# Another order of the Strassen products and down tiles, and the band sums behind two down tiles, in a two-layer hybrid trunk

## The chip, the cores and the metric

The kernel runs as one program on one core of a Trainium2 chip. The metric is the device time of one execution in microseconds (us), as the median of several. One execution is also recorded by the profiler; all rows below come from that one.

## What is computed

640 tokens (128 context, 512 latent) of width 1024 go through two layers. Each layer is a mixing part and a dense feed-forward part (FFN), each between two RMS norms with scale, shift and gate from a conditioning vector. Layer 0 mixes by attention and a state space scan, layer 1 by a pooling mixer. What matters here is the FFN, the pooling mixer, and the gate rows:

```python
def modulation(cvec, w_mod, b_mod):
    m = jnp.expand_dims(jax.nn.silu(cvec) @ w_mod + b_mod, -2)
    return split_last(m, (D_MODEL,) * 6)

def swiglu(h, w_gate, w_up, w_down):
    return (jax.nn.silu(h @ w_gate) * (h @ w_up)) @ w_down

# pool_mixer: mean over a window of 2, 4, 8 or 16 tokens, less the token,
# then one 256x256 product for each quarter of the width
    xp = xp + g_p * rmsnorm(mix_p, norm_post_mix[l])
    fp = swiglu(modulate(xp, norm_pre_ffn[l], shf_p, scf_p), ffn_w_gate[l], ffn_w_up[l], ffn_w_down[l])
    xp = xp + gf_p * rmsnorm(fp, norm_post_ffn[l])
```

The FFN is 1024 to 2816 and back. All is float32 in and out.

## The kernel before

Float32 products are made of three matmuls: each operand is split into a high part (tiles named `h..`, or `ah`, `a1h`, by a ScalarE copy, L89 and L588) and a low part (`l..`, `al`, `a1l`, a subtraction, L90 and L589), and high by high, high by low and low by high are summed in PSUM. `net.split` (L86) does it for weights: ScalarE the high part, VectorE (or the engine handed over) the low part. `net.raw` (L71) takes a buffer of a ring of four, named "raw", and loads 128x1024 of a weight into it over the SyncE queue.

`_ffn` (L517) works on 22 tiles of the hidden width, in 11 pairs of a gate and an up matrix. The first pair is "plain": eight products (L97 to L99) whose weights are split up front, low parts on GpSimd, with the last tiles of the work before (`tails`) put between. The other 20 matrices (L514) use a scheme of seven products with half-size operands, p1 to p7, each of 12 matmuls with 320 columns. Products 1, 6, 7 and 4 add up in one PSUM tile A, products 5 and 3 in a tile B; between the steps of A, ScalarE copies what is there (L548 after p1, L558 after p6, L566 after p7), so p6 has to wait for L548, p7 for L558 and p4 for L566. While one matrix is multiplied, the next is prepared: `load` (SyncE), `adds` (four sums on GpSimd, L484 to L487, of two raw tiles into `q` and `t4`), and the splits `a`, `b`, `c`, `d`. Between products stand five calls `d()`: each multiplies one tile of 128 tokens of the pair before with half of its down weights (six matmuls with 512 columns; L97 to L99, added up on VectorE at L611), and lets the background generators go on by a step (`net.bg`). `out_split` (L588, L589) splits the finished hidden tile, on ScalarE and GpSimd.

The background work, `mod_gate_mac`, makes gate rows that are wanted later: for each half it takes four units of 512 KB of `w_mod` through the ring and multiplies and adds them on VectorE (L273, four instructions a unit; "MAC" below). The first FFN has four such halves, the second two.

After the first FFN's loop, `finish0` runs: the last two pairs' down products (`tail`, 48 matmuls for a pair of 128-token tiles, 24 for one), post-norm (`finish_tile`), next pre-norm into `hn`, and the pooling mixer: `pool_in(tt)` multiplies `hn` by a band matrix on TensorE (L1348), `mix(tt)` by the pool weights (L1650) and makes the next pre-norm, whose transposes (L331) lie in `trs`. `_band_shift` (L1363 reduction on VectorE, L1365 a tiny matmul, L1368 eight scalings) makes the shift for `pool_in` out of the band, which is loaded over the ScalarE queue when `finish0` starts.

The code hands instructions to a tile framework that orders those of each engine by its own planning; the order in the code is where it starts from. Every engine runs its own queue; the queue of SyncE carries the weight loads.

Of the kernel before, what the change touches and what calls it, by code (L numbers as in the profile page):

```python
# [9 lines left out]
F32 = mybir.dt.float32  # L10
# [7 lines left out]
P = 128  # L18
# [27 lines left out]
class Net:  # L46
# [211 lines left out]
    def mod_gate_mac(self, dst, l, j, half, gain):  # L258
        nc = self.nc
# [5 lines left out]
        nc.scalar.dma_start(gb, self.t[gain][l, c0 : c0 + 512].partition_broadcast(P))  # L265
        acc = self.mrp.tile([P, 2, 512], F32, tag="macc", name=self.name("macc"), bufs=1)
        for u in range(4):
            x = self.raw(self.t["w_mod"][l, 2 * j + half, u])
            yield
            for k2 in range(2):  # L270
                kc = 2 * u + k2
                for v in range(2):
                    nc.vector.scalar_tensor_tensor(  # L273
                        acc[:, v], x[:, k2 * 512 : k2 * 512 + 512], self.silc[:, kc, v : v + 1],
                        acc[:, v] if kc else bb, op0=ALU.mult, op1=ALU.add,
                    )
                if k2 == 0:
                    yield
        for v in range(2):
            h = self.mrp.tile([P, 512], F32R, tag="modh", name=self.name("modh"), bufs=1)  # L280
            lo = self.mrp.tile([P, 512], F32R, tag="modl", name=self.name("modl"), bufs=1)
# [187 lines left out]
class Matrix:  # L469
# [28 lines left out]
    def d(self, eng=None):  # L498
        self.wd = self.net.split(self.fr, "d", self.t4, eng)
# [17 lines left out]
def _ffn(net, l, A, fr, sp, tails, switch, finish):  # L517
    nc, t = net.nc, net.t
# [73 lines left out]
    def down_load(q, dh):  # L592
        return net.raw(t["w_down"][l, q, dh])
# [19 lines left out]
    g0, u0 = mats(0)  # L613
    g0.load()
    u0.load()
    w0 = {}
    for f in range(2):
        for m, tags in ((g0, "ab"), (u0, "cw")):
            w0[m, f] = net.split(fr, tags[f], (m.ra, m.rb)[f], nc.gpsimd)
    s0 = sp.tile([P, 2, TOK], F32, tag="sg", name=net.name("sg"))  # L620

    def plain(m, f, half):
        out = net.pt([P, HB])
        wh, wl = (x.rearrange("p (k n) -> p k n", k=KC) for x in w0[m, f])
        net.mm3(out, [(wh[:, k], wl[:, k], bh, bl) for k, (bh, bl) in enumerate(A.plain(half))])
        d = s0[:, f, half * HB : half * HB + HB]
        if m is g0:
            nc.scalar.activation(d, out, AF.Silu)
        else:
            nc.vector.tensor_tensor(d, d, out, ALU.mult)  # L630

    plain(g0, 0, 0)
    tails.pop(0)()
    plain(u0, 0, 0)
    tails.pop(0)()
    plain(g0, 1, 0)
    plain(u0, 1, 0)
    plain(g0, 0, 1)
    A.pair(0, 64)
# [23 lines left out]
    for n, m in enumerate(seq, 2):  # L663
        p, up = divmod(n, 2)
        w = Work(m, wg if up else None)
# [8 lines left out]
        def d():  # L674
            if fill:
                down_add(fill.pop(0), up, [(prev, wdn)], p == 1)
            net.bg()
# [4 lines left out]
        w.p2()  # L682
        if final and up:
            last[1, 0] = net.split(fr, "a", down_load(NPAIR - 1, 0), None)
        w.p6()
        d()
        w.p5()
        if nx:
            nx.a()
        w.p7()  # L690
        if nx:
            nx.adds()
# [2 lines left out]
            nx.c()  # L695
        if final and up:
            last[0, 1] = net.split(fr, "c", down_load(NPAIR - 2, 1), None)
        w.p4()
        if up:
            at = [out_split(wg, 0)]  # L700
# [4 lines left out]
        if nx:  # L705
            nx.b()
            nx.d()
        d()
        d()
        if up:  # L710
            if final:
                last[1, 1] = net.split(fr, "b", down_load(NPAIR - 1, 1), None)
# [662 lines left out]
def trunk(ctx: ExitStack, tc: tile.TileContext, t: dict, o: dict):  # L1375
    net = Net(ctx, tc, t, o)
    nc = tc.nc
# [14 lines left out]
    with pool("x0", "right", 2) as xp:  # L1392
# [4 lines left out]
        for tt in range(NT):  # L1397
            x = xp.tile([P, D], F32, tag="x", name=net.name("x"), bufs=NT)
            net.in_dma(tt, x)
            xts.append(x)  # L1400
        a, _ = net.mod_ab_of(0, None, sc, PV_PREMIX)
# [109 lines left out]
    with pool("xg", "right") as xg, pool("wo", "left") as wo:  # L1511
# [31 lines left out]
        for tt in range(NT):  # L1543
# [6 lines left out]
            x = xq.pop(0)  # L1550
# [72 lines left out]
    def finish0(tail, right):  # L1623
# [7 lines left out]
        nc.scalar.dma_start(band, t["band"])  # L1631
        us = pool_weights()
        a = net.mod_ab_of(1, m1[0], m1[1], PV_PREMIX)[0]
        ab = a, _band_shift(net, band, m1[0])
        abf = net.mod_ab_of(1, m1[3], m1[4], PV_PREFFN)
        pfs, trs = {}, []

        def pool_in(tt):
            pfs[tt] = _pool_tile(net, pp, band, hn, tt, ab)

        def mix(tt):
# [21 lines left out]
        def rest():  # L1663
            pool_in(3)
            mix(2)
            trs.pop(0)()
            pool_in(4)
            mix(3)
            trs.pop(0)()
            mix(4)  # L1670
            trs.pop(0)()
            return trs

        return rest
# [122 lines left out]
```

## Time and profile before

| | |
|---|---|
| median of 3 runs | 1468.32 us (1464.43 to 1470.96) |
| the profiled execution | 1471.61 us |
| its span in the trace | 1469.7 us |
| TensorE (PE) busy | 1382.8 us, 94% of the span, 7914 matmuls |
| VectorE (DVE) busy | 1008.8 us, 69% |
| ScalarE (ACT) busy | 642.0 us, 44% |
| GpSimd (POOL) busy | 449.2 us, 31% |
| mean granted clock of TensorE | 0.965 of full |

TensorE is busy nearly all the time, so the rest of the span, some 87 us, is what waits on it add up to, and a granted clock below 1 is time that its matmuls take longer. Of the two levels 0.5 is 1.2 GHz and 1.0 is 2.4 GHz. A figure between them for a stretch is a mean. Brackets at the end of a timeline row give the idle time of that engine just before the instruction and what released it.

### The profile page before, as it was taken

What the parts mean: (1) busy time and instruction counts of PE and PEld (TensorE: products, weight loads), DVE (VectorE), ACT (ScalarE), POOL (GpSimd) and SP (SyncE); (2) the same over time, 40 slices, a digit from 0 to 9 for tenths busy, and PEclk for the clock granted to TensorE, in tenths of its full rate; (3) what the DMA queues carried; (4) which work ended last, traced back from release to release, by engine and by line L of the source; (5) the groups of instructions that cost most, each with busy time, mean ns of one, the idle gap of its engine ahead of it and who ended that gap; (6) DMA issues with size and microseconds to landing.
All of it is one profiled execution on the core that took longest, in us unless ns stands there. A gap on an engine that the chain in (4) does not pass through costs nothing.

```text
span 1469.7 us, 20410 instructions
## 1 busy us (share of the span) xinstructions
PE 1382.8 (94%) x7914; PEld 1181.7 (80%) x7914; DVE 1008.8 (69%) x1460; ACT 642.0 (44%) x1138; POOL 449.2 (31%) x357
## 2 busy tenths in 40 slices
PE   5999999999998989899999998697999999999998
PEld 2888765667567978798899998597998899999996
DVE  3755547777747886887876666476878766666657
ACT  3545634744325544333333434256553333433443
POOL 0000133354300544335253333022442433333320
PEclk9999999999999999999999999787999999999999
DMA  9433435600063242333232224321242332222213
GB/s 366 134 129 126 139 136 188 201 29 1 29 215 115 94 142 81 115 122 115 94 129 87 87 86 144 130 86 43 66 134 91 113 115 86 87 87 79 79 58 143
DMA packets 50276, 165.45 MB, mean 113 GB/s; under 512 B 5938, under 2 KB 9522, under 8 KB 50052
## 3 DMA queue, kind: packets, MB, share of 16 engines
q1 hardware_dynamic: 43344, 153.96, 31.1%
q10 hardware_dynamic: 6836, 10.19, 2.1%
q8 instruction: 62, 1.02, 0.3%
q14 instruction: 34, 0.28, 0.1%
HBM read 155.57 MB, written 8.56 MB: 112 GB/s over the span
## 4 chain that ended last, share of the span: by engine, by line
PE 45%; DVE 10%; issue 4%; POOL 4%; DMA 3%; ACT 2%; POOLq 0%; DVEq 0%; ACTq 0%; SPq 0%
PE ps L514 25%; PE ps L99 6%; PE ps L97 6%; PE ps L98 6%; DVE macc L273 3%; PE ps L1348 2%; POOL al L589 1%; PE ps L1650 1%; DVE a2l L421 1%; DMA raw<-in_w_mod 1%; DMA band<-in_band 1%; DVE y L611 1%; DVE la L90 1%; POOL q L484 1%; POOL q L485 1%
## 5 line engine op out<-in xcount | busy, mean ns | idle before, releaser
L484 POOL TENSOR_TENSOR q<-raw,raw 128x512 f32<-128x512 f32 x40 | 57.8, 1444 | 389.1 <-DVE lc L90 207.5
L99 PE MATMUL ps<-hw,al 128*128 128x512 f32 x380 | 151.8, 399 | 4.1 <-POOL al L589 4.0
L611 DVE TENSOR_TENSOR y<-y,ps 128x512 f32<-128x512 f32 x180 | 120.8, 681 | 50.3 <-PE ps L99 49.6
L97 PE MATMUL ps<-hw,ah 128*128 128x512 f32 x380 | 152.3, 401 | 0.0
L98 PE MATMUL ps<-lw,ah 128*128 128x512 f32 x380 | 152.1, 400 | 0.1
L514 PE MATMUL ps<-a2h,hc 128*128 128x320 f32 x320 | 101.2, 316 | 11.0 <-ACT sg L548 11.0
L589 POOL TENSOR_TENSOR al<-sg,ah 128x640 fp32r<-128x640 f32 x42 | 75.7, 1806 | 94.9 <-ACT ah L588 94.9
L514 PE MATMUL ps<-a2h,lc 128*128 128x320 f32 x320 | 101.1, 316 | 0.0
L514 PE MATMUL ps<-a2l,hc 128*128 128x320 f32 x320 | 100.9, 315 | 0.0
L514 PE MATMUL ps<-a2h,hb 128*128 128x320 f32 x320 | 99.0, 309 | 0.0
L514 PE MATMUL ps<-a1h,ha 128*128 128x320 f32 x320 | 98.9, 309 | 0.0
L514 PE MATMUL ps<-a1h,la 128*128 128x320 f32 x320 | 98.8, 309 | 0.0
L514 PE MATMUL ps<-a1l,ha 128*128 128x320 f32 x320 | 98.8, 309 | 0.0
L514 PE MATMUL ps<-a2l,hb 128*128 128x320 f32 x320 | 98.8, 309 | 0.0
L514 PE MATMUL ps<-a2h,lb 128*128 128x320 f32 x320 | 98.8, 309 | 0.0
L90 DVE TENSOR_TENSOR lc<-q,hc 128x1024 fp32r<-128x1024 f32 x40 | 51.2, 1279 | 60.7 <-ACT hc L89 60.7
L99 PEld LDWEIGHTS ps<-hw,al 128*128 128x128 f32 x380 | 72.4, 190 | 23.4 <-POOL al L589 6.1
L89 ACT ACTIVATE hc<-q 128x1024 fp32r<-128x1024 f32 x40 | 42.4, 1059 | 96.2 <-PE ps L514 79.2
L98 PEld LDWEIGHTS ps<-lw,ah 128*128 128x128 f32 x380 | 72.6, 191 | 10.8 <-DVE lw L90 0.5
L97 PEld LDWEIGHTS ps<-hw,ah 128*128 128x128 f32 x380 | 72.7, 191 | 10.2
L273 DVE SCALAR_TENSOR_TENSOR macc<-raw,silc,macc 128x512 f32<-128x512 f32 x84 | 74.4, 923 | 5.6 <-DMA raw<-in_w_mod 5.6
L89 ACT ACTIVATE hb<-raw 128x1024 fp32r<-128x1024 f32 x44 | 46.6, 1060 | 66.4 <-issue 33.4
(449 smaller groups left out, 4010.3 us busy)
## 6 DMA issues: line engine op xcount, KB each, us to landing
raw<-in_w_mod SPq DMA_DIRECT2D x80, 512.0 KB, 3.8
raw<-in_w_gate SPq DMA_DIRECT2D x44, 512.0 KB, 3.6
raw<-in_w_up SPq DMA_DIRECT2D x44, 512.0 KB, 3.7
raw<-in_w_down SPq DMA_DIRECT2D x44, 512.0 KB, 4.3
mraw<-in_w_mod SPq DMA_DIRECT2D x16, 512.0 KB, 10.2
xs<-xd SPq DMA_DIRECT2D x10, 512.0 KB, 8.3
x<-in_x_sample SPq DMA_DIRECT2D x8, 512.0 KB, 7.5
raw<-in_w_xbc SPq DMA_DIRECT2D x8, 512.0 KB
```

Of the source, the lines that this page charges most:

```text
L89: self.nc.scalar.activation(h, x, AF.Copy)
L90: (eng or self.nc.vector).tensor_tensor(l, x, h.bitcast(F32), ALU.subtract)
L97: mm(out, ah, bh, start=first and i == 0, stop=False)
L98: mm(out, ah, bl, start=False, stop=False)
L99: mm(out, al, bh, start=False, stop=last and i == n - 1)
L273: nc.vector.scalar_tensor_tensor(acc[:, v], x[:, k2 * 512 : k2 * 512 + 512], self.silc[:, kc, v : v + 1], acc[:, v] if kc else bb, op0=ALU ...
L421: eng.tensor_tensor(l, x, h.bitcast(F32), ALU.subtract)
L484: g.tensor_tensor(self.q[:, lo], self.rb[:, lo], self.ra[:, lo], ALU.subtract)
L514: mm(out, x[:, k], z[:, k], start=first and n == 0, stop=n == len(terms) - 1, skip_group_check=True)
L589: (eng or nc.gpsimd).tensor_tensor(al, g.s[:, f], ah.bitcast(F32), ALU.subtract)
L611: nc.vector.tensor_tensor(yd, yd, out, ALU.add)
L1348: nc.tensor.matmul(o, x, m, start=i == 0, stop=i == len(mats) - 1, skip_group_check=True)
```

## The change

Five edits. The seven products and five down tiles stand in another order: before p1 p2 p6 d p5 p7 d p4 d p3 d d, now p1 p2 p5 p6 d d p7 d p4 d p3 d (the splits of the next matrix keep their places among them, but for `a`, `b` and `d`). The gate rows' units have a buffer of their own, one (`mraw`), and give control back once before their first MAC more and once more behind the last. The first pair's four splits are made one by one, ahead of the product that needs them, with low parts on VectorE. `_band_shift` is called by the first `pool_in`, after the tails of two tiles. In `rest`, the third set of transposes stands ahead of `mix(4)`.

```diff
--- before.py
+++ after.py
@@ -265,7 +265,9 @@
         nc.scalar.dma_start(gb, self.t[gain][l, c0 : c0 + 512].partition_broadcast(P))
         acc = self.mrp.tile([P, 2, 512], F32, tag="macc", name=self.name("macc"), bufs=1)
         for u in range(4):
-            x = self.raw(self.t["w_mod"][l, 2 * j + half, u])
+            x = self.mrp.tile([P, 1024], F32, tag="mraw", name=self.name("mraw"), bufs=1)
+            nc.sync.dma_start(x, self.t["w_mod"][l, 2 * j + half, u])
+            yield
             yield
             for k2 in range(2):
                 kc = 2 * u + k2
@@ -274,8 +276,7 @@
                         acc[:, v], x[:, k2 * 512 : k2 * 512 + 512], self.silc[:, kc, v : v + 1],
                         acc[:, v] if kc else bb, op0=ALU.mult, op1=ALU.add,
                     )
-                if k2 == 0:
-                    yield
+                yield
         for v in range(2):
             h = self.mrp.tile([P, 512], F32R, tag="modh", name=self.name("modh"), bufs=1)
             lo = self.mrp.tile([P, 512], F32R, tag="modl", name=self.name("modl"), bufs=1)
@@ -614,9 +615,10 @@
     g0.load()
     u0.load()
     w0 = {}
-    for f in range(2):
-        for m, tags in ((g0, "ab"), (u0, "cw")):
-            w0[m, f] = net.split(fr, tags[f], (m.ra, m.rb)[f], nc.gpsimd)
+
+    def first(m, f, tag):
+        w0[m, f] = net.split(fr, tag, (m.ra, m.rb)[f])
+
     s0 = sp.tile([P, 2, TOK], F32, tag="sg", name=net.name("sg"))
 
     def plain(m, f, half):
@@ -629,11 +631,15 @@
         else:
             nc.vector.tensor_tensor(d, d, out, ALU.mult)
 
+    first(g0, 0, "a")
     plain(g0, 0, 0)
+    first(u0, 0, "c")
     tails.pop(0)()
     plain(u0, 0, 0)
+    first(g0, 1, "b")
     tails.pop(0)()
     plain(g0, 1, 0)
+    first(u0, 1, "w")
     plain(u0, 1, 0)
     plain(g0, 0, 1)
     A.pair(0, 64)
@@ -682,11 +688,12 @@
         w.p2()
         if final and up:
             last[1, 0] = net.split(fr, "a", down_load(NPAIR - 1, 0), None)
+        w.p5()
         w.p6()
-        d()
-        w.p5()
         if nx:
             nx.a()
+        d()
+        d()
         w.p7()
         if nx:
             nx.adds()
@@ -695,6 +702,7 @@
             nx.c()
         if final and up:
             last[0, 1] = net.split(fr, "c", down_load(NPAIR - 2, 1), None)
+        d()
         w.p4()
         if up:
             at = [out_split(wg, 0)]
@@ -705,8 +713,6 @@
         if nx:
             nx.b()
             nx.d()
-        d()
-        d()
         if up:
             if final:
                 last[1, 1] = net.split(fr, "b", down_load(NPAIR - 1, 1), None)
@@ -1631,11 +1637,13 @@
         nc.scalar.dma_start(band, t["band"])
         us = pool_weights()
         a = net.mod_ab_of(1, m1[0], m1[1], PV_PREMIX)[0]
-        ab = a, _band_shift(net, band, m1[0])
+        ab = [a]
         abf = net.mod_ab_of(1, m1[3], m1[4], PV_PREFFN)
         pfs, trs = {}, []
 
         def pool_in(tt):
+            if len(ab) == 1:
+                ab.append(_band_shift(net, band, m1[0]))
             pfs[tt] = _pool_tile(net, pp, band, hn, tt, ab)
 
         def mix(tt):
@@ -1667,8 +1675,8 @@
             pool_in(4)
             mix(3)
             trs.pop(0)()
+            trs.pop(0)()
             mix(4)
-            trs.pop(0)()
             return trs
 
         return rest
```

In the changed kernel the line numbers move by 1 to 8 (L548 becomes L549, L588 becomes L589, L273 becomes L275, L1363 becomes L1369).

ScalarE, at the border between two pairs of the first FFN: `ah` are the high parts of the pair that is done, L548 the copy of A after p1 of the next matrix. Before:

```order
L588 ACTIVATE ah_5890<-sg_5583 128x640
L290 DMA gd<-macc_5383 1x512
L89 ACTIVATE hb_5925<-raw_5772 128x1024
L265 DMA gb_5942<-in_npost_mix 128x512
L588 ACTIVATE ah_5921<-sg_5583 128x640
L89 ACTIVATE hw_5961<-raw_5959 128x1024
L548 ACTIVATE sg_5965<-ps_5970 128x320
L264 DMA bb_6474<-in_b_mod 1x512
```

Now:

```order
L89 ACTIVATE hd_5915<-t_1086_5839 128x512
L589 ACTIVATE ah_5879<-sg_5556 128x640
L89 ACTIVATE hw_5921<-raw_5919 128x1024
L89 ACTIVATE hb_5911<-raw_5743 128x1024
L549 ACTIVATE sg_5925<-ps_5930 128x320
L589 ACTIVATE ah_5907<-sg_5556 128x640
L89 ACTIVATE ha_5985<-raw_5926 128x1024
```

The copy after p1 (now L549) has moved ahead of the second `ah`, and the down weights' `hw` ahead of `hb`.

VectorE, at the end of the first FFN: the low parts of the last pair, then the additions of the tails (`y<-y,ps`), the band's reduction, and `hn` of tile 0. Before:

```order
L90 TENSOR_TENSOR lb_8370<-raw_8367,hb_8369 128x1024
L589 TENSOR_TENSOR al_8364<-sg_8121,ah_8363 128x640
L1363 TENSOR_REDUCE rs_8423<-band 128x4
L1368 TENSOR_SCALAR mv_8427<-mv_1567,ps_8425 128x2 x8
L611 TENSOR_TENSOR y<-y,ps_8437 128x512
L350 TENSOR_TENSOR junk_8451<-y,G_8379 128x512
L352 TENSOR_SCALAR ss_1494_8452<-ss_1494_8452 128x1
```

Now, from the third addition of the tails on:

```order
L351 TENSOR_TENSOR junk_8488<-y,G_8379 128x512
L353 TENSOR_SCALAR ss_1491_8439<-ss_1491_8439 128x1
L612 TENSOR_TENSOR y<-y,ps_8494 128x512
L351 TENSOR_TENSOR junk_8488<-y,G_8379 128x512
L1369 TENSOR_REDUCE rs_8524<-band 128x4
L105 RECIPROCAL r_8462<-sd_8461 128x1
L1374 TENSOR_SCALAR mv_8528<-mv_1567,ps_8526 128x2
L365 SCALAR_TENSOR_TENSOR xs_8385<-junk_8438,r_8462,xs_8385 128x512 x2
L353 TENSOR_SCALAR ss_1502_8489<-ss_1502_8489 128x1
L1374 TENSOR_SCALAR mv_8528<-mv_1567,ps_8526 128x2 x7
L105 RECIPROCAL r_8470<-sd_8469 128x1
L316 TENSOR_SCALAR hn<-xs_8385,r_8470 128x1024
```

The reduction moved from ahead of the first addition to behind the fourth, and stays ahead of `hn`.

VectorE, in the first gate matrix of the first FFN: MACs of the second and third unit (`raw_4958` and `raw_5002` before, `mraw_4974` and `mraw_5128` now). Before:

```order
L273 SCALAR_TENSOR_TENSOR macc_4881<-raw_4958,silc,macc_4881 128x512 x4
L90 TENSOR_TENSOR lc_4932<-q_4915,hc_4931 128x1024
L273 SCALAR_TENSOR_TENSOR macc_4881<-raw_5002,silc,macc_4881 128x512
L567 TENSOR_TENSOR sg_4821<-sg_4821,ps_4884 128x320
L273 SCALAR_TENSOR_TENSOR macc_4881<-raw_5002,silc,macc_4881 128x512 x3
L90 TENSOR_TENSOR ld_4979<-t_943_4916,hd_4978 128x512
```

Now:

```order
L90 TENSOR_TENSOR la_4882<-raw_4822,ha_4881 128x1024
L90 TENSOR_TENSOR lc_4940<-q_4923,hc_4939 128x1024
L275 SCALAR_TENSOR_TENSOR macc_4898<-mraw_4974,silc,macc_4898 128x512 x4
L568 TENSOR_TENSOR sg_4821<-sg_4821,ps_4855 128x320
L275 SCALAR_TENSOR_TENSOR macc_4898<-mraw_5128,silc,macc_4898 128x512 x3
L90 TENSOR_TENSOR ld_4995<-t_944_4924,hd_4994 128x512
```

Between the last MAC of one unit and the first of the next stood a split (`lc`); now a short addition stands there.

## Rows read from the trace of the kernel before

**Rows 1.** Stages: us; busy PE, PEld, DVE, ACT, POOL; clock, DMA share, GB/s.

```profile
560.00:754.00 194.00, 182.43 (x1034) 166.51 (x1033) 156.64 (x191) 70.21 (x101) 80.43 (x48) 0.97 0.34 110
754.00:908.00 154.00, 154.00 (x928) 144.32 (x927) 97.19 (x116) 61.41 (x87) 51.53 (x38) 1.00 0.31 99
1040.00:1150.00 110.00, 105.22 (x622) 97.41 (x620) 90.61 (x101) 49.68 (x72) 47.37 (x29) 0.98 0.35 114
```

**Rows 2.** Waits of PE, whole span: waiting, releaser, total us, times, longest.

```profile
PE ps L1365 <- DVE rs L1363: 14.4, 1, 14.4
PE ps L514 <- ACT sg L548: 11.0, 4, 4.9
PE ps L97 <- DVE a1h L431: 7.6, 1, 7.6
...
PE ps L97 <- ACT ha L89: 3.6, 1, 3.6
```

**Rows 3.** Waits of PE, 545 to 760 us (first FFN, MAC stretch).

```profile
PE ps L514 <- ACT sg L566: 4.1, 2, 3.1
PE ps L514 <- ACT sg L548: 4.0, 2, 2.1
PE ps L99 <- POOL al L589: 3.3, 3, 1.5
```

**Rows 4.** Timeline, ACT, 598 to 617 us: start, length, operation [idle, releaser].

```profile
601.62 0.74 ACT L588 ACTIVATE ah<-sg 128x640 fp32r<-128x640 f32 x1 [3.74 <-DVE sg L579]
...
603.21 0.42 ACT L548 ACTIVATE sg<-ps 128x320 f32<-128x320 f32 x1
```

**Rows 5.** Timeline, DVE, 582 to 610 us.

```profile
600.77 0.81 DVE L579 TENSOR_TENSOR sg<-sg,sg 128x640 f32<-128x640 f32 x1
```

**Rows 6.** Timeline, POOL, 560 to 705 us.

```profile
581.77 1.29 POOL L484 TENSOR_TENSOR q<-raw,raw 128x512 f32<-128x512 f32 x1 [16.90 <-DMA raw<-in_w_gate]
```

**Rows 7.** Page, part 5: busy us, mean ns, idle before with its releaser.

```profile
L589 POOL TENSOR_TENSOR al<-sg,ah 128x640 fp32r<-128x640 f32 x42 | 75.7, 1806 | 94.9 <-ACT ah L588 94.9
...
L90 DVE TENSOR_TENSOR lc<-q,hc 128x1024 fp32r<-128x1024 f32 x40 | 51.2, 1279 | 60.7 <-ACT hc L89 60.7
```

**Rows 8.** Table by stage, the 10 us around one wait of the MAC stretch.

```profile
610.00:620.00 10.00, 6.87 (x30) 5.74 (x29) 8.18 (x10) 2.96 (x5) 2.88 (x2) 0.83 0.35 109
```

**Rows 9.** Page, part 6: DMA issues, count, KB each, us to landing.

```profile
raw<-in_w_mod SPq DMA_DIRECT2D x80, 512.0 KB, 3.8
```

**Rows 10.** Waits of PE, 1040 to 1400 us (second FFN).

```profile
PE ps L514 <- ACT sg L548: 2.1, 1, 2.1
PE ps L514 <- ACT sg L566: 2.0, 2, 1.6
```

**Rows 11.** Timeline, PE, between the two FFNs.

```profile
928.24 0.59 PE L1365 MATMUL ps<-rs,cm 128*128 128x4 f32 x2 [14.45 <-DVE rs L1363]
...
945.63 1.60 PE L1348 MATMUL ps<-band,hn 128*128 128x128 f32 x12 [3.11 <-DVE hn L315]
```

**Rows 12.** Timeline, DVE, 912 to 948 us.

```profile
917.76 0.81 DVE L589 TENSOR_TENSOR al<-sg,ah 128x640 fp32r<-128x640 f32 x1
927.50 0.69 DVE L1363 TENSOR_REDUCE rs<-band 128x4 f32<-128x512 f32 x1 [8.93 <-DMA band<-in_band]
...
942.56 0.69 DVE L611 TENSOR_TENSOR y<-y,ps 128x512 f32<-128x512 f32 x1
```

**Rows 13.** Timeline, POOL, 960 to 1024 us.

```profile
970.95 2.81 POOL L90 TENSOR_TENSOR la<-raw,ha 128x1024 fp32r<-128x1024 f32 x1
```

**Rows 14.** Table by stage, between the two FFNs.

```profile
914.00:928.00 14.00, 0.00 (x0) 0.00 (x0) 5.04 (x5) 1.47 (x2) 2.76 (x2) 0.60 0.96 355
...
946.00:978.00 32.00, 32.00 (x181) 27.88 (x180) 26.30 (x47) 19.66 (x48) 9.45 (x4) 1.00 0.16 52
```

**Rows 15.** Timeline, ACT, 510 to 522 us.

```profile
518.20 0.74 ACT L588 ACTIVATE ah<-sg 128x640 fp32r<-128x640 f32 x1 [2.67 <-DVE sg L630]
```

**Rows 16.** Timeline, PE, 1000 to 1022 us.

```profile
1007.68 1.89 PE L1650 MATMUL ps<-q,pf 128*128 128x256 f32 x8
```

## The prediction

> **What bounds the kernel now.** I read the waits of TensorE first, then a table by stage, then the queues of the engines that TensorE waits for. The table [rows 1] shows two kinds of stretch inside the same loop over matrices. Between 754 and 908 us TensorE is busy for all of 154.00 us at full clock (1.00); between 560 and 754 us, the same loop with background multiply-accumulates (MACs, L273) on VectorE beside it, it is busy for 182.43 of 194.00 us at 0.97, and VectorE works 156.64 us there. So the loop has nothing to give where VectorE is light, and the time to be had lies in its waits. These are few [rows 2]: 14.4 us once for the band sums, 11.0 us in four waits for the copy L548 (the longest 4.9), 7.6 us once for the first operand of layer 1's FFN, 3.6 us for the first weight of layer 0's. In the first MAC stretch they are 4.1, 4.0 and 3.3 us [rows 3], 11.4 in all.
>
> How such a wait arises: ScalarE stood 3.74 us for the low-priority `ah` of the pair just ended, and the copy that TensorE wanted (L548, after p1) came behind it, at 603.21 us [rows 4]. `ah` waited for VectorE's L579 at 600.77 us [rows 5], late behind MACs. Upstream of it, GpSimd's sums for the next matrix once stood 16.90 us for a weight load [rows 6]: the MAC loads share four buffers with the weights.
>
> **The change, part by part.** The sum is made against the profiled execution (1471.61 us), which lies 3.3 us above the median, so 3.3 comes off at the end.
>
> *Order of products, first FFN.* TensorE does the same matmuls, so nothing is added; what moves is who is late. In the new ScalarE order the copy after p1 stands ahead of the second `ah`, so p6 no longer hangs on L579, and p5 runs before p6 too: the 4.0 us [rows 3] should go. For L566, 4.1 us, the new order puts two down tiles instead of one between the copy and p4 (six more matmuls, under 1.7 us by the 13.7 us of 48 tail matmuls below), and the weights' buffers are freer; I take half, 2.0. For `al` I take nothing: counted from the end of p3, the first down tile that reads it used to follow two old down tiles and three products and now follows four products, so it comes rather earlier, while a low part takes 1.81 us on GpSimd [rows 7]. Each wait also leaves a restart: a window of 10 us with one shows a granted clock of 0.83 instead of 1.00 [rows 8], so 3.4 us at half rate, which costs 1.7; three windows of this stretch show it, 5.1 in all, of which I take 3.0 with the waits. Sum 9; bounds 2 (the L548 waits are half filled by what is late next, `al`) and 16.5 (11.4 and 5.1).
>
> *Modulation rows in their own buffer, more background steps.* This adds and removes no MAC; per half 22 steps instead of 14 spread 16 MACs. It frees the ring of four for weights, which is what [rows 6] waits for. But one buffer serves all units, so a unit's load starts only after the last MAC of the unit before it. A load takes 3.8 us to land [rows 9]. The VectorE rows of the first gate matrix show four MACs of one unit and three of the next with one short addition between: there VectorE will stand for about 3.8 us, once in each FFN. VectorE is 81% busy in such a stretch [rows 1], so most of it is slack; in other places splits and additions stand between. The SyncE queue also holds weight loads behind a waiting MAC load; the weights are wanted a matrix later, so I cost it at nothing; if that cover is gone, GpSimd's sums are late next, then `hc`, then p5.
>
> *Second FFN's MAC stretch.* Its waits are 2.1 and 2.0 us [rows 10], half as many MACs, VectorE 90.61 of 110 us [rows 1]. By the same shares: 2.1 and 0.9 of restart, 3. Bounds 0 and 6.
>
> *Band sums behind two down tiles.* Now TensorE's queue has the little matmul L1365 ahead of the tails; it waits for the band's load, and TensorE stands 14.45 us, to 928.24 [rows 11]. The reduction itself starts when the band has landed, 927.50 [rows 12]. In the new order the tails need only the last low part, which ended at 917.76 + 0.81 = 918.6 [rows 12]. Before, 48 tail matmuls took from 928.8 to the last addition at 942.56 [rows 12], 13.7 us with their half-rate start; nine of them now run ahead of the end of p3, so 39 are left: 11.1 us, last addition at about 929.7. VectorE's new order puts the reduction and the eight scalings behind that addition and ahead of `hn` of tile 0, so after it come its product (0.7), the reduction (0.69), matmul, update of x, square and `hn`: about 6.5 us against 3.1 before (945.63 less 942.56 [rows 11, 12]). pool_in(0) starts at 936.2 rather than 945.6: 9.4 less. The nine early matmuls push the end of p3 by 1.6 (2.1 less 0.5 into a wait), and the new 6.5 us of idle time before pool_in(0) brings one more restart, 1.7. I take 6. Bounds: 2 (the restart lasts over pool_in(0) and its neighbours) and 11 (`hn` not held up by the reduction). Its cover for the load of the band: the tails; without them the old 14.45 is back.
>
> That `hn` waits its turn is why 6.5 and not 3.1 is counted. VectorE stood 8.93 us at the reduction [rows 12] and ran nothing behind it; but nothing behind it was ready then, so the row alone doesn't decide. The Trainium skill, Perfetto Trace Analysis, section Tensor Engine Instruction, says that ScalarE, VectorE and GpSimd start their instructions strictly in order. By that rule the band brings 6; without it 6 + 3.4, about 9.
>
> *First splits one by one, on VectorE.* Low parts go from GpSimd (2.81 us each beside VectorE [rows 13]) to VectorE (1.28 [rows 7]). In the second FFN's start TensorE is busy throughout that stretch (946 to 978 us, 32.00 of 32.00 [rows 14]), so nothing. At the first FFN's start TensorE waited 3.6 [rows 2] for `ha`, which I leave; the 4.9 for L548 came from an `ah` at 518.20 [rows 15] ahead of it. It goes, but `al` of that same tensor is wanted by the first down tile about 2.5 us later. I take 3; bounds 0 and 5.
>
> *Transposes ahead of mix(4).* TensorE's wait of 7.6 [rows 2] comes because the last transposes stood behind mix(4), whose first eight matmuls take 1.89 [rows 16], all sixteen about 3.6. Moved, mix(4) fills 3.6 of the wait and the operand comes 3.6 sooner; but its ScalarE and VectorE work then meets the first plain products. I take 2: bounds 7.6 (all of it) and -4 (mix(4) at half rate and its work in the operand's way).
>
> Sum 9 + 3 + 6 + 3 + 2 = 23: 1448.6 in the terms of the profiled run, **1445** on the median. Its own range: 1437 to 1453.
>
> **Rivals.** (a) *Waits move instead of going*: VectorE has no less to do, and the next late row (`al`, L566) takes over. Then the loops bring 3 together, the band 5, the starts 0: 1463.6, 1460 on the median. For it: 156.64 of 194 us. Against: the stall followed above came from the order of ScalarE's queue. (b) *All MAC waits and restarts go*, as in the quiet stretch: 16.5 + 6 + 6 + 3 + 2 = 33.5: 1435. For it: a ring free of MAC loads; against: MACs are still bunched. (c) *`hn` overtakes the reduction*: 3.4 more, 1442; against it the VectorE order. (d) *Slower by the clock*: pool_in(0) now starts after idle time; if the clock then stays at half over the 32.00 us of work that had 1.00 [rows 14], 32 us come back: 1480.6 less 3.3, 1477. It decides from 23 us at half. Against: before, it was full in that stretch although TensorE had done nothing from 914 to 928 us [rows 14]. (e) *Slower by the single buffer*: if all 24 units cost VectorE 3.8 us, the first stretch's 16 take 61 of its 37 free us and the second's 8 take 30 of its 19; 35 us fall on TensorE, the loops' 12 don't come, 11 remain: 1495.6, 1492 on the median; it decides from 2.8 us for each unit. Against: in most places two or more splits stand between units. (f) *Nothing moves*: 1468.
>
> **Numbers.** Forecast 0.45, (a) 0.22, (b) 0.13, (c) 0.05, (d) 0.06, (e) 0.05, (f) 0.04. About 0.5%, 7.3 us, is what a measurement of this kernel can tell from no change: faster means below 1461. Forecast, (b), (c) and most of (a) lie there, 0.80; the rest of (a) and (f) 0.12; (d), (e) 0.08. The range goes from 1431, under (b), to 1462, over (a).
>
> **What would show it.** Right: no wait of TensorE on the band reduction; its tails start some 5 us after p3; a wait of 5 to 7 us for `hn`; no p6 wait on `ah`; MAC stretches near 1.00. Wrong: MACs with idle time released by the modulation load, weight loads late behind them, half clock past 936 us, or a 7 us wait still at the second FFN's start.

## The result, and the profile after

The changed kernel takes 1448.39 us (median of 4 runs, 1447.63 to 1449.88), beside 1469.64 us of the kernel before (4 runs): a ratio of 0.9862, 95% interval 0.9834 to 0.9890. The profiled execution took 1448.13 us, 23.5 less than the profiled one before. The forecast was 1445, with a range of 1431 to 1462. So the total came out close, but the parts that made it did not: that is what this section and the runs below show.

TensorE's busy time fell from 1382.8 to 1370.3 us with the same 7914 matmuls, at a mean granted clock of 0.978 instead of 0.965. So of the 23.4 us by which the span shrank, 12.5 are busy time that shrank, and 10.9 are waits that went.

Waits of TensorE in the changed kernel, whole span (waiting, releaser, total us, times, longest), to be laid beside [rows 2]:

```profile
PE ps L515 <- ACT sg L549: 12.2, 5, 6.4
...
PE ps L332 <- DVE y L316: 4.3, 2, 2.7
PE ps L1354 <- DVE hn L316: 4.3, 1, 4.3
PE ps L97 <- DVE a1h L432: 4.1, 1, 4.1
PE ps L97 <- ACT ha L89: 3.6, 1, 3.6
PE ps L99 <- POOL al L590: 3.3, 4, 0.9
PE ps L1371 <- DVE rs L1369: 3.2, 1, 3.2
```

The wait for the band sums is down from 14.4 to 3.2 us, and 4.3 for `hn` have come; the wait for the second FFN's operand went from 7.6 to 4.1, with 4.3 for `y` (the transposes) new beside it. The wait of p6 for the copy after p1, which was to go, has grown from 11.0 to 12.2.

Where the 23.5 us came from is read at landmarks that both programs have: the start of p1 of the first and of the 19th matrix in each FFN's loop, and the start of the first pool tile (945.63 and 917.69 us). Times are differences of start times in the two timelines.

| stretch | before, us | after, us | change | forecast |
|---|---|---|---|---|
| start to first matrix of the first FFN's loop | 510.7 | 506.3 | -4.4 | -3 |
| first FFN's loop, 18 matrices | 377.3 | 365.0 | -12.3 | -9 |
| 19th matrix to the first pool tile | 57.6 | 46.4 | -11.2 | -6 |
| first pool tile to the second FFN's loop | 107.1 | 104.8 | -2.3 | -2 |
| second FFN's loop, 18 matrices | 356.5 | 362.2 | +5.7 | -3 |
| the rest, to the end of the execution | 62.4 | 63.4 | +1.0 | 0 |

Stages after (us; busy PE, PEld, DVE, ACT, POOL; clock, DMA share, GB/s), to be read beside [rows 1]: the MAC stretch of the first FFN, the quiet one behind it, and the first matrices of the second FFN.

```profile
555.00:750.00 195.00, 192.14 (x1125) 176.58 (x1124) 147.91 (x182) 72.08 (x106) 71.54 (x51) 1.00 0.33 106
750.00:890.00 140.00, 139.74 (x837) 130.38 (x836) 101.34 (x127) 57.56 (x83) 48.61 (x33) 1.00 0.33 107
1030.00:1130.00 100.00, 95.25 (x537) 87.42 (x538) 70.45 (x83) 43.32 (x65) 38.03 (x28) 0.97 0.31 101
```

The MAC stretch is nearly quiet now: 192.14 of 195.00 us busy at clock 1.00, where it was 182.43 of 194.00 at 0.97. Its waits, of which three groups of [rows 3] had added up to 11.4 us, are these (two more are of 0.6 and 0.3):

```profile
PE ps L99 <- POOL al L590: 0.9, 1, 0.9
PE ps L515 <- DVE sg L568: 0.6, 1, 0.6
...
PE ps L515 <- ACT sg L549: 0.4, 1, 0.4
```

The second FFN's loop is the loss. Its first two matrices took 26.9 and 22.0 us, where they had taken 20.3 and 20.0, 8.6 more; the other 16 took 2.9 less. The first FFN's first matrix shows the same thing, 28.3 us, where it had taken 27.1. ScalarE there:

```profile
509.73 1.05 ACT L89 ACTIVATE hw<-raw 128x1024 fp32r<-128x1024 f32 x1
517.36 0.23 ACTq L264 DMA_DIRECT2D bb<-in_b_mod  x1
517.64 0.44 ACT L549 ACTIVATE sg<-ps 128x320 f32<-128x320 f32 x1 [6.86 <-POOL bb L263]
```

ScalarE's queue came to a load of 2 KB of bias (L264, for the second half of the gate rows), and stood 6.86 us; the copy after p1 (L549), which p6 of TensorE waited for, was the next behind it. The load waited for a memset on GpSimd:

```profile
508.77 2.29 POOL L485 TENSOR_TENSOR q<-raw,raw 128x512 f32<-128x512 f32 x1
...
514.36 2.51 POOL L488 TENSOR_TENSOR t<-raw,q 128x512 f32<-128x512 f32 x1
516.81 0.52 POOL L263 MEMSET bb<- 128x512 f32 x1
```

The memset itself takes 0.52 us; it stood behind four sums for the next matrix. The prediction had weighed what the copy would no longer stand behind, and not what else had moved in front of it. In the second FFN the same chain costs 4.6 us where before there was no such wait. GpSimd and ScalarE of the changed kernel:

```profile
1029.64 0.52 POOL L263 MEMSET bb<- 128x512 f32 x1
1030.55 1.06 ACT L89 ACTIVATE hw<-raw 128x1024 fp32r<-128x1024 f32 x1 [6.56 <-POOL bb L263]
```

and GpSimd of the kernel before:

```profile
1044.88 0.53 POOL L263 MEMSET bb<- 128x512 f32 x1 [3.75 <-DVE a2l L421]
```

Before, the memset stood ahead of the four sums, the first of which started at 1049.86; now it stands behind them (1021.04 to 1029.69).

### The profile page after: what moved, and what is told of

Read it like the earlier page. It is cut to its first block, busy times and chain, and to the rows that moved or that the text cites. A ratio compares the mean times of both kernels' runs of the same rounds, so it can differ in the third digit from the quotient of the medians.

```text
span 1446.3 us, 20387 instructions
## 1 busy us (share of the span) xinstructions
PE 1370.3 (95%) x7914; PEld 1172.8 (81%) x7914; DVE 984.5 (68%) x1468; ACT 639.0 (44%) x1140; POOL 415.9 (29%) x349
## 4 chain that ended last, share of the span: by engine, by line
PE 74%; DVE 10%; DMA 6%; issue 4%; ACT 3%; POOL 2%; POOLq 0%; ACTq 0%; DVEq 0%; SPq 0%
PE ps L515 26%; PE ps L97 11%; PE ps L99 11%; PE ps L98 11%; DMA mraw<-in_w_mod 3%; PE ps L179 3%; DVE macc L275 3%; PE ps L1354 2%; PE ps L1255 1%; PE ps L1658 1%; PE ps L1237 1%; DMA band<-in_band 1%; PE ps L1217 1%; PE ps L1238 1%; PE ps L1239 1%
## 5 line engine op out<-in xcount | busy, mean ns | idle before, releaser
L485 POOL TENSOR_TENSOR q<-raw,raw 128x512 f32<-128x512 f32 x40 | 54.9, 1372 | 362.7 <-DMA raw<-in_w_up 117.2
L99 PE MATMUL ps<-hw,al 128*128 128x512 f32 x380 | 151.2, 398 | 1.8 <-POOL al L590 1.8
L612 DVE TENSOR_TENSOR y<-y,ps 128x512 f32<-128x512 f32 x180 | 121.1, 683 | 39.1 <-PE ps L99 36.5
L515 PE MATMUL ps<-a2h,hc 128*128 128x320 f32 x320 | 100.8, 315 | 12.2 <-ACT sg L549 12.2
L275 DVE SCALAR_TENSOR_TENSOR macc<-mraw,silc,macc 128x512 f32<-128x512 f32 x84 | 79.3, 972 | 28.0 <-DMA mraw<-in_w_mod 28.0
L488 POOL TENSOR_TENSOR t<-raw,q 128x512 f32<-128x512 f32 x40 | 58.5, 1464 | 100.0 <-DVE ld L90 65.8
L98 PEld LDWEIGHTS ps<-lw,ah 128*128 128x128 f32 x380 | 72.2, 190 | 12.2
L89 ACT ACTIVATE hd<-t 128x512 fp32r<-128x512 f32 x40 | 25.3, 632 | 120.6 <-PE ps L515 105.9
```

The source lines that it names most:

```text
L98: mm(out, ah, bl, start=False, stop=False)
L99: mm(out, al, bh, start=False, stop=last and i == n - 1)
L275: nc.vector.scalar_tensor_tensor(acc[:, v], x[:, k2 * 512 : k2 * 512 + 512], self.silc[:, kc, v : v + 1], acc[:, v] if kc else bb, op0=ALU ...
L485: g.tensor_tensor(self.q[:, lo], self.rb[:, lo], self.ra[:, lo], ALU.subtract)
L488: g.tensor_tensor(self.t4, self.ra[:, hi], self.q[:, hi], ALU.subtract)
L515: mm(out, x[:, k], z[:, k], start=first and n == 0, stop=n == len(terms) - 1, skip_group_check=True)
```

## The experiments

Medians are of the runs of each kernel; the ratio is to the kernel before, measured beside it. The changed kernel was run again beside three of the runs below (neither order nor buffer, one by one on GpSimd, all three edits): 1450.28 us (1447.6 to 1451.24), ratio 0.9890 (0.9851 to 0.9928). So the base is 1448 to 1450, and differences under some 3 us can't be told by medians. Across groups of runs it is more: the kernel before itself had medians from 1462.86 to 1469.64 us beside them. There the ratio is the safer guide, 0.9862 and 0.9890 for the changed kernel.

> The changed kernel itself, as a base on the same chip as the runs beside it: 1447 to 1450.

**Undoing one part.** Four runs take one part back from the changed kernel, and one takes two.

*Old order of the products.* Edit:

```diff
-        w.p5()
         w.p6()
+        d()
+        w.p5()
         if nx:
             nx.a()
-        d()
-        d()
         w.p7()
...
```

> The changed kernel with the old order of products and down tiles (p1 p2 p6 d p5 p7 d p4 d p3 d d), all else kept. Theory (the order takes p6 out of the way of the pair's high part): waits of p6 for the copy after p1 come back in the first MAC stretch, 3 to 5 us, and the time is 5 to 9 us above the changed kernel, about 1455. Rival (the modulation units' own buffer alone did it): MAC stretch as quiet as now, time within 2 us of 1448.

Measured: 1456.32 us (1452.37 to 1462.73), ratio 0.9929 (0.9906 to 0.9952). The theory's time held, its place only in part: in the MAC stretch the copy after p1 costs 2.4 us in three waits, and p4's wait for the copy after p7 2.8 in one. The first FFN's loop takes 372.3 us in the trace against 365.0, 3.5 of it in one matrix (25.4 against 21.9).

*Units back in the ring of four.* Edit:

```diff
-            x = self.mrp.tile([P, 1024], F32, tag="mraw", name=self.name("mraw"), bufs=1)
-            nc.sync.dma_start(x, self.t["w_mod"][l, 2 * j + half, u])
-            yield
+            x = self.raw(self.t["w_mod"][l, 2 * j + half, u])
             yield
...
```

> The changed kernel with the gate rows' units back in the ring of four and two background steps a unit, all else kept. Theory (ring shared with weights makes GpSimd's sums late): waits of p4 or p7 on copies behind hc come back, 3 to 6 us more, about 1452. Rival (the order of products alone did it): MAC stretch stays quiet, within 2 us of 1448; VectorE's waits for the unit's load (28 us in all now) go away and cost TensorE nothing.

Measured: 1463.16 us (1458.92 to 1471.29), ratio 0.9977 (0.9946 to 1.0009): 13 to 15 us above the changed kernel, far over the 3 to 6 expected, and with another wait than named. The edit takes back the two more background steps of a unit as well (one of them in the lines left out), so the run doesn't part the buffer from the steps. TensorE's longest wait in the MAC stretch:

```profile
PE ps L99 <- POOL al L589: 9.9, 4, 3.3
```

It is the pair's low part `al`, 9.9 us in four waits, that holds the first down tile back. GpSimd once:

```profile
595.12 1.30 POOL L484 TENSOR_TENSOR q<-raw,raw 128x512 f32<-128x512 f32 x1 [1.13 <-DMA raw<-in_w_up]
...
600.42 1.71 POOL L487 TENSOR_TENSOR t<-raw,q 128x512 f32<-128x512 f32 x1
602.09 1.98 POOL L589 TENSOR_TENSOR al<-sg,ah 128x640 fp32r<-128x640 f32 x1
```

The sums start when a weight load lets them (595.12), and `al` follows them at 602.09, so here the shared ring makes `al` late; the other three waits were not followed. The new order asks for `al` earlier.

*Neither order nor buffer.* Both edits above together, with band, first splits and transposes as in the changed kernel:

> The changed kernel with the old order of products and the gate rows' units back in the ring: what the band, the first splits and the transposes bring by themselves. With the order alone at 1463 and the buffer alone at 1456, theory (the two need each other: the new order wants the pair's low part earlier, and only free weight buffers let GpSimd make it in time): 1452 to 1457, so that the order without the buffer is a loss and the buffer without the order is worth little. Rival (each gives its own part): the two single losses, 15 and 8 us, add up to about 1471.

Measured: 1452.04 us (1448.10 to 1453.95), ratio 0.9898 (0.9852 to 0.9944). It lies in the theory's range and far from the rival's 1471: with both, 1448 to 1450; with the buffer alone 1456; with the order alone 1463; with neither 1452. The order by itself loses 11 us against neither. The buffer by itself is 4 above, and the intervals of the two ratios overlap, so its loss isn't shown. Together they bring some 2 us, measured side by side (1452.04 and 1450.28), less than the medians can tell. The run's MAC stretch has waits like those of [rows 3]:

```profile
PE ps L514 <- ACT sg L548: 4.0, 2, 2.0
PE ps L99 <- POOL al L589: 3.4, 3, 1.5
PE ps L514 <- ACT sg L566: 2.4, 2, 1.4
```

In the trace the first FFN's loop takes 374.6 us against 365.0, so 9.6 more, while its start takes 2 us less and the second FFN's loop 362.7 against 362.2.

*Band shift ahead of the tails again.* Edit:

```diff
-        ab = [a]
+        ab = [a, _band_shift(net, band, m1[0])]
```

> The changed kernel with the band's shift made before the first tail tile, as before. Theory (tails hide the band's load): one wait of TensorE of 13 to 15 us for the reduction comes back and the time is 10 to 12 us above the changed kernel, about 1459. Rival (the load of the band holds pool_in anyway): 6 us or less, since pool_in(0) moves by less than the tails do.

Measured: 1461.39 us (1457.16 to 1466.61), ratio 0.9965 (0.9941 to 0.9989): 11 to 13 us above the changed kernel. TensorE:

```profile
912.88 0.59 PE L1371 MATMUL ps<-rs,cm 128*128 128x4 f32 x2 [14.09 <-DVE rs L1369]
...
929.29 3.16 PE L1354 MATMUL ps<-band,hn 128*128 128x128 f32 x16 [3.11 <-DVE hn L316]
```

The wait is 14.09 us again, and the first pool tile starts at 929.29, where the changed kernel has:

```profile
912.84 0.59 PE L1371 MATMUL ps<-rs,cm 128*128 128x4 f32 x2 [3.23 <-DVE rs L1369]
917.69 1.22 PE L1354 MATMUL ps<-band,hn 128*128 128x128 f32 x4 [4.26 <-DVE hn L316]
```

*mix(4) ahead of the third transposes again.*

```diff
-            trs.pop(0)()
             trs.pop(0)()
             mix(4)
+            trs.pop(0)()
```

> The changed kernel with mix(4) ahead of the third set of transposes again. Theory (mix(4) fills the wait): the wait for the first operand of the second FFN grows from 4.1 to about 7.6 us and the time by 2 to 3 us. Rival (the waits that came for y and the low part of the operand give it back): within 1 us, no difference that can be told.

Measured: 1446.98 us (1444.58 to 1452.15), ratio 0.9863 (0.9815 to 0.9911): no difference that can be told, and if any, faster. In the profiled execution, the slowest of the four, the wait for the operand grew to 9.3 us, past the theory's 7.6; but the stretch from the 19th matrix of the first FFN to the first of the second took 148.7 us, against 151.2 and 148.9 in the two profiles of the changed kernel.

**The first splits.** All four up front, low parts on GpSimd, as before the change; and, to part the two halves of this edit, one by one but on GpSimd:

```diff
-        w0[m, f] = net.split(fr, tag, (m.ra, m.rb)[f])
+        w0[m, f] = net.split(fr, tag, (m.ra, m.rb)[f], nc.gpsimd)
```

> The changed kernel with all four first splits made up front, low parts on GpSimd, as before. Theory (this part is worth the 3.6 us that the first FFN's start gained): 1 to 4 us more, about 1451, with a wait for a low part on GpSimd back at the first plain product. Rival (nothing waits on it): within 1 us.

> The changed kernel with the first pair's four splits still made one by one, but their low parts on GpSimd. Theory (low parts on GpSimd stretch VectorE's work beside them, which makes hn late and leaves TensorE with band matmuls alone at half clock): the 20 us at half clock in the pooling part come back and the time is 8 to 14 us above the changed kernel, about 1459. Rival (making all four ahead of time is what hurts): within 3 us of the changed kernel.

Measured: up front 1461.14 us (1455.91 to 1464.69), ratio 0.9978 (0.9956 to 1.0000); one by one on GpSimd 1459.58 us (1453.03 to 1462.95), ratio 0.9956 (0.9928 to 0.9983). Both are 9 to 13 us above the changed kernel, far over the 1 to 4 expected of the first: a part that the prediction priced at 3 us, and at nothing in the pooling stretch. So it is the engine, not the moment.

By the landmarks of the table above, the profile of one by one on GpSimd is 3.3 us longer than the changed kernel's up to the first FFN's loop, 4.4 in the first two matrices of that loop, 3.4 between the first pool tile and the second loop (5.9 against the changed kernel's second profile), and 2.4 in the first two matrices of the second loop; the other stretches differ by 0.2 or less. Around the first FFN's start TensorE waits longer, 9.6 us for the copy after p1 instead of 6.4, and 1.6 for a low part on GpSimd. In the pooling part it doesn't wait longer; there it is the clock. First the kernel before:

```profile
978.00:998.00 20.00, 20.00 (x83) 18.83 (x83) 10.10 (x21) 6.08 (x16) 1.27 (x1) 0.51 0.21 75
```

then the changed kernel:

```profile
953.00:961.00 8.00, 8.00 (x35) 7.25 (x35) 4.04 (x8) 1.63 (x6) 0.00 (x0) 0.57 0.29 109
```

and the one with low parts on GpSimd:

```profile
957.00:981.00 24.00, 24.00 (x113) 22.52 (x113) 12.72 (x23) 8.23 (x24) 3.93 (x2) 0.57 0.24 85
```

TensorE is busy for all of these stretches; it is at half clock for about 20 us in the first and the third and for some 7 in the second. From the first pool tile to the second FFN's loop the granted clock is 0.86 in the kernel before and in both runs with low parts on GpSimd, and 0.91 and 0.92 in the two profiles of the changed kernel. VectorE in the 13 us in which GpSimd makes the low parts (one by one on GpSimd, 948 to 961 us; line, operation, count, busy us, mean ns):

```profile
L365 DVE SCALAR_TENSOR_TENSOR xs<-junk,r,xs 128x512 f32<-128x512 f32 x3 | 4.0, 1376 | 0.0
L351 DVE TENSOR_TENSOR junk<-y,G 128x512 f32<-128x512 f32 x2 | 4.0, 1984 | 0.1
L316 DVE TENSOR_SCALAR hn<-xs,r 128x1024 f32<-128x1024 f32 x1 | 2.7, 2661 | 0.0
L612 DVE TENSOR_TENSOR y<-y,ps 128x512 f32<-128x512 f32 x2 | 1.4, 675 | 0.0
```

and in the 20 us (936 to 956) where the changed kernel has the first three on VectorE:

```profile
L365 DVE SCALAR_TENSOR_TENSOR xs<-junk,r,xs 128x512 f32<-128x512 f32 x4 | 2.8, 746 | 0.0
L351 DVE TENSOR_TENSOR junk<-y,G 128x512 f32<-128x512 f32 x4 | 2.7, 680 | 0.0
L612 DVE TENSOR_TENSOR y<-y,ps 128x512 f32<-128x512 f32 x4 | 2.7, 677 | 0.0
...
L90 DVE TENSOR_TENSOR lw<-raw,hw 128x1024 fp32r<-128x1024 f32 x1 | 1.2, 1217 | 0.0
...
L316 DVE TENSOR_SCALAR hn<-xs,r 128x1024 f32<-128x1024 f32 x1 | 0.7, 745 | 0.0
```

The product L351 and `hn`, which read SBUF, take 1984 and 2661 ns beside GpSimd, and 680 and 745 without; L612, one of whose inputs is PSUM, stays at 675. So the low parts cost VectorE more time on GpSimd (some 6 us in this stretch) than the 4.9 they cost on VectorE itself. The Trainium skill, SBUF — State Buffer, section Who interferes with whom, says that a VectorE instruction with two SBUF inputs contends with a GpSimd instruction that reads SBUF. The trace agrees for L351 and L612; `hn`, which has one large SBUF input, that sentence doesn't cover.

That a late `hn` leaves TensorE with narrow band matmuls, as the expectation has it, isn't shown: TensorE doesn't wait there. What the traces show is that the framework also gave TensorE another order. One by one on GpSimd:

```profile
967.85 8.54 PE L1354 MATMUL ps<-band,hn 128*128 128x8 f32 x40
```

and the changed kernel:

```profile
959.96 0.46 PE L332 MATMUL ps<-cm,y 128*128 128x128 f32 x2
961.45 4.53 PE L1354 MATMUL ps<-band,hn 128*128 128x8 f32 x40
```

The same forty matmuls (of 128 and of 8 columns) take 8.54 us at a clock of 0.50 and 4.53 at 1.00. In the changed kernel transposes (L332) and more of `mix` stand ahead of them; in the kernel before and in both runs on GpSimd they follow six matmuls of `mix` and the band matmuls of the tile before. Whether VectorE's lateness or that order keeps the clock down was not parted. The order alone doesn't fix it: in the changed kernel's second profile, with the same order as in the first, the clock was 1.00 from 950 to 963 us, where the first fell to 0.57.

**The bias loads.** Issued by SyncE instead of ScalarE:

```diff
-        nc.scalar.dma_start(bb[0:1], self.t["b_mod"][l, j * D + c0 : j * D + c0 + 512].unsqueeze(0))
+        nc.sync.dma_start(bb[0:1], self.t["b_mod"][l, j * D + c0 : j * D + c0 + 512].unsqueeze(0))
```

> The changed kernel with the 2 KB bias loads of the gate rows issued by SyncE instead of ScalarE. Theory (the copy after p1 of the first matrix stands behind a bias load that waits for GpSimd's memset, itself behind four sums): the two waits of 6.4 and 4.6 us shrink to what the high part needs, below 2 us each; 8 to 12 us less than the changed kernel, about 1438. Rival (VectorE, full of multiply-accumulates, is what is late, and the bias load only stands in front): the wait passes to the low part of the pair or to a later copy in the same matrix, 3 us or less gained.

Measured: 1447.92 us (1445.52 to 1450.63), ratio 0.9886 (0.9853 to 0.9919). The rival held: the 6.4 us are gone and nothing is won. In the same first stretch TensorE now waits for the down weights' low part:

```profile
PE ps L98 <- DVE lw L90: 4.3, 1, 4.3
```

That low part stands on VectorE behind two MACs and a long split. So the bias load was the last of two late things, and taking it away alone wins nothing.

**The band.** Loaded over SyncE's queue, with the loads of the x tiles behind it in the code instead of ahead:

```diff
-        xs = x_back(ts.enter_context(pool("xs", "left")), 0)
+        xs = ts.enter_context(pool("xs", "left")).tile([P, NT, D], F32, name=net.name("xs"))
...
-        nc.scalar.dma_start(band, t["band"])
+        nc.sync.dma_start(band, t["band"])
+        for tt in range(NT):
+            nc.sync.dma_start(xs[:, tt], xd[0, tt])
```

> The changed kernel with the band loaded over the SyncE queue after three of the five x tiles instead of over ScalarE's queue behind two gate loads. Theory (what is left at the pooling start is the band's landing, 911.9 us, 13 us after p3): the reduction starts some 4 to 6 us sooner, the waits of 3.2 and 4.3 us shrink to 2 to 3 us together, 4 to 6 us less, about 1443. Rival (VectorE's order holds hn of tile 0 behind the reduction whatever the band does): the wait for hn stays above 4 us and 2 us or less are gained.

Measured: 1445.27 us (1442.20 to 1446.46), ratio 0.9863 (0.9827 to 0.9898). The reduction started only 0.9 us sooner, so the theory of the landing falls. But the framework now put the update of x (L365) ahead of the reduction:

```profile
908.94 1.42 DVE L365 SCALAR_TENSOR_TENSOR xs<-junk,r,xs 128x512 f32<-128x512 f32 x2
...
911.17 0.69 DVE L1369 TENSOR_REDUCE rs<-band 128x4 f32<-128x512 f32 x1 [0.15 <-DMA band<-in_band]
```

and the wait for `hn` shrank from 4.26 to 1.42 us:

```profile
911.90 0.39 PE L1371 MATMUL ps<-rs,cm 128*128 128x4 f32 x2 [2.35 <-DVE rs L1369]
913.71 3.79 PE L1354 MATMUL ps<-band,hn 128*128 128x128 f32 x16 [1.42 <-DVE hn L316]
```

The pool tile starts 4.0 us sooner, 0.9 of it from the earlier reduction. That comes near the rival (c) of the prediction, priced there at 3.4, though `hn` itself still runs behind the reduction; it is the update of x that has passed it. For the whole kernel a gain isn't shown: the ratio is that of the changed kernel.

**Together.** Bias loads over SyncE with mix(4) first:

> Bias loads issued by SyncE and mix(4) ahead of the third transposes again, all else as in the changed kernel. If the two are independent: the gain of the bias loads alone and 1 to 2 us more, about 1437. If the wait at the second FFN's first matrix depends on when its plain products start, the two gains overlap and it is no faster than the bias loads alone.

Measured: 1444.22 us (1442.82 to 1445.20), ratio 0.9860 (0.9831 to 0.9888): not the 1437 of independent gains, and by the ratio no gain over the changed kernel that can be told. And all three:

> Three edits on the changed kernel together: bias loads over SyncE, the band over SyncE ahead of two x tiles, mix(4) ahead of the third transposes again. If they are independent: the band's 3 us, the transposes' 1 to 2 and the bias loads' 0 to 1, about 1442 beside 1448 of the changed kernel. If the first matrix of the second FFN takes it back: 1445 or more.

Measured: 1439.74 us (1436.88 to 1442.80), ratio 0.9819 (0.9787 to 0.9851), beside the changed kernel's 1450.28: all its runs are below all of the changed kernel's. It is the fastest version found, and its gain, 10.5 us, is more than the 4 to 6 that the single gains had promised. Between the 19th matrix of the first FFN and the second FFN's loop it takes 147.0 us, and for the second loop 359.0 against 362.2.

## Why the prediction was right, and where it was not

**Total and direction.** 1448.39 lies in the range and 3 us from the forecast. But the terms, 9 + 3 + 6 + 3 + 2, were wrong one by one and their errors cancelled: that the sum came out is luck. By the runs, order and buffer brought some 2 us where 12 were forecast, the band 11 to 13 for 6, the first splits 9 to 13 for 3, and the transposes nothing or a loss for 2. One sum of the prediction is off without bearing on the rest: the chances of (d) and (e), 0.06 and 0.05, make 0.11 and not 0.08.

**Order and buffer, first FFN (9), second (3).** The mechanism in the loop was right, and the size near: the waits for L548 and L566 are all but gone from the MAC stretch, with 12.3 us less in the first loop, 9.6 by the run with neither. But it took both edits: "For `al` I take nothing" was true only with the buffer in place; without it, `al` costs 9.9 us. And what the pair gains in the later matrices it gives back at the starts. Against the profile with neither, the last 16 of the 18 matrices are 11.3 us shorter in the first loop and 2.9 in the second, while the first two are 1.7 and 2.3 longer and the stretch up to the first loop 2.0. There the waits moved instead of going, as rival (a) has it. The second loop, forecast 3 us shorter, is 5.7 longer than before; its last 16 matrices are 2.9 shorter, as forecast, and its first two 8.6 longer, where TensorE stands 6.8 us instead of 1.1 and is at half clock for 6.8 more.

**The single buffer, rival (e).** The waits foreseen are there. The page's group of MACs (busy us, mean ns, idle before and its releaser):

```profile
L275 DVE SCALAR_TENSOR_TENSOR macc<-mraw,silc,macc 128x512 f32<-128x512 f32 x84 | 79.3, 972 | 28.0 <-DMA mraw<-in_w_mod 28.0
```

VectorE stood 28.0 us for unit loads, some 1.2 for each of 24 units, under the 2.8 from which the rival would have decided. Outside the first matrices TensorE hardly waits in the MAC stretch: VectorE had that time to spare.

**Band (6).** The term measured 11 to 13. The order in VectorE's queue and the added wait for `hn` came as written:

```profile
909.64 0.69 DVE L612 TENSOR_TENSOR y<-y,ps 128x512 f32<-128x512 f32 x1 [0.80 <-PE ps L99]
...
912.10 0.69 DVE L1369 TENSOR_REDUCE rs<-band 128x4 f32<-128x512 f32 x1 [1.04 <-DMA band<-in_band]
...
913.61 1.41 DVE L365 SCALAR_TENSOR_TENSOR xs<-junk,r,xs 128x512 f32<-128x512 f32 x2
...
916.88 0.75 DVE L316 TENSOR_SCALAR hn<-xs,r 128x1024 f32<-128x1024 f32 x1
```

The last addition (909.64), then the reduction, then x and `hn`. Two things were mis-sized. The tails began right behind p3, at 898.7 us, since some of them need no low part of the last tile; so there was no restart at half clock for them. And the reduction didn't follow the last addition at once, but waited 1.04 us more for the band, so that the load is still what comes last. The last addition and pool_in(0) lie 8.1 us apart, where 6.5 were forecast. The wait behind the reduction was worth 3.4 in the prediction; in the run with x ahead of the reduction the pool tile came 4.0 sooner, or 3.1 without the 0.9 of the earlier reduction.

The reciprocal `r` that x needs waits for `sd` of ScalarE, which was done at 910.51:

```profile
910.21 0.30 ACT L104 ACTIVATE sd<-ss 128x1 f32<-128x1 f32 x1
```

Yet VectorE stood idle for the band until 912.10 and ran `r` behind the reduction, at 912.70. This agrees with the rule quoted from the Trainium skill, Perfetto Trace Analysis, section Tensor Engine Instruction (strict order).

**First splits (3 and nothing).** The largest miss: 9 to 13 us. The first FFN's start, priced at 3, brought 3.3 us up to the loop and 4.4 in its first two matrices, by the run with low parts on GpSimd. But "It goes", said of the 4.9 us for L548 there, failed: a 2 KB load had moved in front of the copy, and the wait is 6.4. The second FFN's start, priced at nothing, brought 3.4 to 5.9 us between the first pool tile and the loop, and 2.4 in the first two matrices. "TensorE is busy throughout that stretch" was read from a row that ends at 978 us, at a clock of 1.00; the next 20 us, just as busy, were at 0.51, and busy time at half clock is time that can be won.

**Transposes (2).** Measured as -1 to -3, or nothing: the operand did come sooner, and a wait of 4.3 us for `y` came in return. The lower bound of the term had named mix(4)'s work in the operand's way; whether it is that was not followed.

**The signs named.** Of those for right, the MAC stretch at 1.00 came. The wait for `hn` was 4.3 us instead of 5 to 7, one of 3.2 on the reduction was left, and the tails began behind p3 at once and not 5 us later. Of those for wrong, at least two came without deciding: VectorE's idle time for the units' loads, and half clock past 936 us (at 953 us, for some 7 us).

**What stays open.** Why the second FFN's loop is longer was not settled: with any one part undone, and with order and buffer both undone, it takes 362 to 365 us in the trace, against 356.5 before. The memset behind the sums is one late thing, but with the bias load moved to SyncE the loop still takes 362.7. Another thing seen is VectorE, which at the first matrix runs two splits of the second operand and one of weights at 2.3 to 2.6 us each beside GpSimd's sums; in the kernel before, two of the three also took 1.9 and 2.2. A second buffer for the units was not tried.

## What to carry to other kernels

Price an edit of an engine's load by the clock as well as by the busy share, and in the stretch behind the one it touches too: a TensorE that is busy at half clock has time to be won. Two edits that look independent, an order that wants something earlier and a buffer that lets it come earlier, have to be tried in all four combinations; here the order alone lost 11 us. A total that comes out doesn't show that its terms did. And when a compute instruction moves forward in a queue, read what else now stands in front of it, small loads with a wait above all.

## What the runs showed of the hardware

Work moved from GpSimd to VectorE made VectorE less busy, 984.5 us busy in the changed kernel and 993.5 in the one by one on GpSimd: a low part costs 1.2 us on VectorE, while on GpSimd it takes 2.8 us and stretches VectorE's own instructions beside it by a factor of 2.9 (L351) to 3.6 (`hn`). A DMA that ScalarE issues, and that waited for GpSimd, held up ScalarE's compute behind it for 6.86 us. And TensorE at 20.00 of 20.00 us busy was granted a clock of 0.51 while it ran matmuls of 128 and 8 columns, with some fourteen of 256 among them.
